# A conditioned convolution / RWKV-7 / product-key layer on one core: order of the second convolution, early second-half activations, loads and stores around the first output projection

## The chip, the core and the metric

The kernel runs on one core of a Trainium2 chip, in one launch. The metric is the device time of an execution in microseconds; what is compared is the median of repeated runs.

The core has five engines with instruction queues of their own: TensorE (PE; its weight loads are listed as PEld), VectorE (DVE), ScalarE (ACT), GpSimd (POOL) and SyncE (SP), which issues nearly all DMAs here. Each engine takes its instructions strictly in the order in which they stand in the program; a DMA waits in SP's queue until what it needs is there, and the DMAs behind it wait too.

## The reference, cut to what matters

```python
mod = silu(c) @ cond_w + cond_b                       # six vectors of 1024: shift1, scale1, gate1, shift2, scale2, gate2
h = layer_norm(x) * (1 + scale1) + shift1             # x: 1024 tokens x 1024
p = h @ w_in                                          # 2816 columns
# group A: 1024 of the columns: gated, a causal depthwise convolution of 31 taps over time, layer norm, silu
u = p[:, :512] * sigmoid(p[:, 512:1024]);  y_conv = silu(layer_norm(conv31(u) + conv_b, g, b))
# group B: 1792 columns: RWKV-7, eight heads of 64
xm = p_rw + (previous token's p_rw - p_rw) * mu;  r, k, v, wd, ad, gd = split(xm)
decay, a, g = f(tanh(wd) @ rw_w2), sigmoid(rw_a0 + ad @ rw_a2), sigmoid(gd) @ rw_g2
kk = k * rw_kk;  kk = kk / max(norm(kk, per head of 64), 1e-12)       # the key norms
k = k * (1 + (a - 1) * rw_ka)
S_t = S_{t-1} diag(w_t) - (S_{t-1} kk_t)(kk_t * a_t)^T + v_t k_t^T;  y_t = S_t r_t
y_rw = (group_norm(y) + sum(r * k * rw_rk) * v) * g
y1 = concatenate(y_conv, y_rw) @ w_out
x1 = layer_norm(2**0.25 * x + gate1 * y1, ln1_g, ln1_b)
# product keys: 8 heads, two halves of 128 keys each, the best 16 of each, the best 16 of their sums
h2 = layer_norm(x1) * (1 + scale2) + shift2;  q = h2 @ peer_wq;  s1, s2 = q @ k1, q @ k2
experts, gates = top 16 of (top 16 of s1 + top 16 of s2), softmax
y2 = sum over the chosen of gelu(h2 . peer_u[e]) * gate * peer_v[e]   # 16384 experts
out = layer_norm(2**0.25 * x1 + gate2 * y2, ln2_g, ln2_b)
```

All is float32. Large products are made of three matmuls over a high and a low part of each operand (`hi`, `lo`, type float32r); smaller ones are plain float32.

## The kernel before, in words

**Stages.** The 1024 tokens are split into two halves of 512 for the input projection and into eight tiles of 128 for the rest.

1. `inproj(0, ...)` works on the first half. `load_x` brings in four tiles of x, `normalize` takes out mean and deviation, `to_channels` transposes a column block of 128 channels for all four tiles on PE, applies shift and scale on ACT (`hf`) and splits the result into the activations `hi` and `lo` (`hhi`, `hlo`; eight blocks each, `k` = 0 to 7). The 22 weight tiles of `w_in` (128 columns each; 24 matmuls of 128x512 for each, `proj`, line 217) are loaded raw, split by ACT and POOL and stored split in DRAM for the second half. `glu` makes the convolution's input and queues `conv(0)`; `products(ct)` and `mixed(ct)`, for four channel groups `ct`, make the operands of the recurrence and store them (`AR_d`, `BK_d`, `v_d`, `bv_d`, `gt_d`). `mixed` makes the key norms: `ones_h`, a block-diagonal matrix of ones, times the squares `sq` on PE gives the sums of squares already spread over the 64 channels of a head; ACT takes the root (`nr`, 128x512), DVE bounds it, takes the reciprocal (line 456) and multiplies.
2. The recurrence runs over 16 steps of 64 tokens: `solve(c)` inverts the step's triangular system (lines 655 to 739), `pass_state(c)` carries the state on (line 760 writes the new state `SN`), `group_norm(j)` finishes 128 tokens at every second step and stores them (`rwkv_d[j]`, line 812).
3. Beside the recurrence runs everything else, as generators in the list `side`: first `inproj(1)` for the second half (its activations are made at its beginning, its `glu` stands at its end), then `front(t0)` for pairs of tiles (loads both groups' outputs, splits them, projects with `w_out`, line 867, adds x, norms twice), then `query(t0)` (`wq`, line 217 with `h2hi`, `h2lo`; the keys' scores, line 939; the best 16 by DVE). `fill()`, called after each few matmuls of the recurrence, steps `side` at a given rate. A second list, `slow`, is stepped once in four fills: the convolutions of both halves, and `choose`, which picks the experts of a tile.
4. `gate_matrix` builds the dense gate matrices of five tiles (masks on DVE, line 1091; matmuls, line 1105) and stores them in DRAM.
5. The expert stage: 32 groups of 512 experts over those five tiles (lines 1388 and 1404), and beside it a gather of single expert rows for the other three tiles.

**What sets the order.** The generators set the program's order, and with it each instruction's priority. A scheduler then places the instructions of every engine: the one of the highest priority that is ready by its own reckoning goes first, and a tile from a pool is given out when a slot is free. The outcome is one fixed list for each engine. What is free or not in the pools therefore decides too: `page(...)` takes from 30 pages of 128x512 (`pgp`), `tp(...)` in `inproj(0)` from 28 others (`tpg`), `mm()` from three PSUM banks, `fe` weights from two buffers.

**Names used below.** `conv(h)` loads its input (`u_d` to `u`), multiplies by taps (`ctap`: made by POOL for the first half and kept in DRAM as `tape_d`; loaded from there for the second), 144 matmuls (line 525), then a norm over channels (lines 534, 543) and its store `conv_d`. `cond_some` brings in rows of `cond_w` (`cw`, 512 KB each, two buffers of the pool `fe`) and DVE multiplies and sums them (line 300) into `mod`. `firsts` lists the generators that have to be finished at step 9, when the pool `fe` is closed. `CD` says whether the second convolution goes to `held` (run from `side`) or to `slow`.

## Time and profile before

| what | value |
|---|---|
| median of 3 runs | 3153.32 us (3149.43 to 3163.98) |
| the profiled execution | 3159.3 us, of which the instructions span 3157.5 us; mean granted clock of TensorE 0.959 |
| PE busy | 2966.5 us, 94% of the span |
| DVE, ACT, POOL busy | 76%, 37%, 57% |
| chain that ended last | PE 52%, DVE 19%, DMA 7% |
| HBM | 800.76 MB read, 141.39 MB written |

The page of the profile gives such totals; the chain is the work that ended last, followed back from the end to what released it. Tables by stage give, for each stretch of the span, its length, the busy time of each engine with its count of records, the granted clock (PEclk, 1.0 is full speed), the busy share of the DMA engines and what they moved. In rows of the timeline the first two numbers are start and length in us, and the bracket at the end is the engine's idle time before the row with what ended it. One float32 matmul of the program leaves two records in the trace, one of type float32r leaves one.

### The profile page before, as it was taken

The page shows a single profiled execution, that of the slowest core. Times are in us where ns is not written, and L with a number is a line of the kernel's source. Part 1 is how long each engine was busy: PE and PEld are TensorE (multiplying, and loading weights), DVE is VectorE, ACT ScalarE, POOL GpSimd, SP SyncE. Part 2 cuts the span into 40 slices and gives each one's busy share as a digit, 9 for nine tenths or more (in the row PEclk, how much of TensorE's full clock was granted, in tenths as well). Part 3 has the DMA queues.
Part 4 walks back from the last instruction along what each step waited for, and adds up shares of the span by engine and source line. Part 5 has one row for each costly group of instructions (what it writes and reads, how often), then busy time and mean ns, then how long its engine had stood idle before and what let it go on. Part 6 is the DMA issues. An engine that isn't in the chain of part 4 may idle for free.

```text
span 3157.5 us, 54845 instructions
## 1 busy us (share of the span) xinstructions
PE 2966.5 (94%) x20416; PEld 2621.4 (83%) x20416; DVE 2388.5 (76%) x5388; ACT 1181.8 (37%) x2220; POOL 1815.5 (57%) x1419
## 2 busy tenths in 40 slices
PE   6979999989899889899999999999999999999996
PEld 4748667878778788898898888889899998999985
DVE  6276654447876989369989999887787877778789
ACT  5552442334345667742332323323222232222323
POOL 2433112224362443477777776877778678777874
PEclk9989999968888999999999999999999999999998
DMA  8878856768576998999999998999999989998995
GB/s 317 308 203 311 261 159 205 267 220 312 201 239 208 310 330 288 292 341 343 312 326 332 318 341 305 341 348 336 345 331 340 341 317 361 327 348 328 339 332 198
DMA packets 441579, 945.77 MB, mean 300 GB/s; under 512 B 92464, under 2 KB 242400, under 8 KB 419296
## 3 DMA queue, kind: packets, MB, share of 16 engines
q1 hardware_dynamic: 248480, 497.62, 45.8%
q0 software_dynamic: 110592, 402.70, 34.9%
q10 hardware_dynamic: 82240, 41.94, 4.8%
q8 instruction: 160, 2.62, 0.3%
q14 instruction: 107, 0.88, 0.1%
HBM read 800.76 MB, written 141.39 MB: 298 GB/s over the span
## 4 chain that ended last, share of the span: by engine, by line
PE 52%; DVE 19%; DMA 7%; issue 6%; POOL 4%; ACT 3%; SPq 0%; another core or an unknown queue 0%; ACTq 0%; POOLq 0%; DVEq 0%
PE mg L1388 18%; PE md L1404 17%; PE mm L217 5%; DVE grow L1267 3%; PE mm L867 2%; POOL grow L1259 2%; PE mm L525 2%; PE mgate L1105 2%; DVE gy L1274 2%; DMA cw<-cond_w 1%; DVE yacc L1422 1%; DMA grow<-peer_u,eid 1%; DVE mask L1091 1%; DMA vraw<-peer_vt 1%; DMA grow<-peer_v,eid 1%
## 5 line engine op out<-in xcount | busy, mean ns | idle before, releaser
L1388 PE MATMUL mg<-h2h,uhi 128*128 128x320 f32 x2024 | 626.9, 310 | 7.1 <-DVE al L1394 7.1
L1388 PE MATMUL mg<-h2h,ulo 128*128 128x320 f32 x2024 | 625.8, 309 | 1.8 <-POOL ulo L1304 1.6
L1388 PE MATMUL mg<-h2l,uhi 128*128 128x320 f32 x2024 | 626.0, 309 | 0.0
L1274 DVE SCALAR_TENSOR_TENSOR gy<-grow,gz,gy 128x1024 f32<-128x1024 f32 x381 | 487.7, 1280 | 18.0 <-DMA grow<-peer_v,eid 16.4
L1404 PE MATMUL md<-vhi,ah 128*128 128x512 f32 x1260 | 486.5, 392 | 5.8 <-ACT ah L1393 2.8
L1404 PE MATMUL md<-vlo,ah 128*128 128x512 f32 x1260 | 491.8, 391 | 0.0
L1404 PE MATMUL md<-vhi,al 128*128 128x512 f32 x1260 | 491.3, 391 | 0.0
L1267 DVE SCALAR_TENSOR_TENSOR grow<-grow,gh 128x1024 f32<-128x1024 f32 x384 | 460.8, 1211 | 36.9 <-DMA grow<-peer_u,eid 32.9
L1259 POOL DMA_INDIRECT grow<-peer_u,eid x384 | 362.5, 944 | 196.3 <-DVE grow L1267 73.7
L1259 POOL DMA_INDIRECT grow<-peer_v,eid x384 | 367.4, 957 | 185.3 <-DVE gy L1274 89.3
L1388 PEld LDWEIGHTS mg<-h2h,uhi 128*128 128x128 f32 x2024 | 380.4, 188 | 15.1 <-DVE al L1394 10.0
L1388 PEld LDWEIGHTS mg<-h2l,uhi 128*128 128x128 f32 x2024 | 380.4, 188 | 5.4
L1388 PEld LDWEIGHTS mg<-h2h,ulo 128*128 128x128 f32 x2024 | 380.3, 188 | 5.5 <-POOL ulo L1304 2.7
L1304 POOL TENSOR_TENSOR ulo<-uraw,uhi 128x1024 fp32r<-128x1024 f32 x128 | 310.0, 2422 | 34.8 <-ACT uhi L1302 29.1
L1304 POOL TENSOR_TENSOR vlo<-vraw,vhi 128x1024 fp32r<-128x1024 f32 x128 | 308.9, 2414 | 10.6 <-ACT vhi L1302 5.4
L1302 ACT ACTIVATE vhi<-vraw 128x1024 fp32r<-128x1024 f32 x128 | 135.2, 1056 | 425.1 <-DMA vraw<-peer_vt 382.7
L1422 DVE TENSOR_TENSOR yacc<-md,yacc 128x512 f32<-128x512 f32 x300 | 204.2, 685 | 115.9 <-PE md L1404 104.3
L1404 PEld LDWEIGHTS md<-vhi,ah 128*128 128x128 f32 x1260 | 236.5, 188 | 53.8 <-ACT ah L1393 4.3
L1404 PEld LDWEIGHTS md<-vlo,ah 128*128 128x128 f32 x1260 | 236.9, 188 | 49.1
L1098 POOL TENSOR_TENSOR ob<-mask,selt 128x384 f32<-128x384 bf16 x160 | 140.9, 894 | 237.9 <-DVE mask L1091 105.3
L1404 PEld LDWEIGHTS md<-vhi,al 128*128 128x128 f32 x1260 | 237.0, 188 | 45.2
L217 PE MATMUL mm<-hhi,wsplit 128*128 128x512 f32 x672 | 228.7, 414 | 8.4 <-ACT gsig L396 5.4
(415 smaller groups left out, 5660.6 us busy)
## 6 DMA issues: line engine op xcount, KB each, us to landing
uraw<-peer_ut SPq DMA_DIRECT2D x128, 512.0 KB
vraw<-peer_vt SPq DMA_DIRECT2D x128, 512.0 KB
wsplit<-split_wq SPq DMA_DIRECT2D x48, 1024.0 KB
G_d<-stage ACTq DMA_DIRECT2D x20, 2048.0 KB
gmat<-G_d SPq DMA_DIRECT2D x32, 1024.0 KB
cw<-cond_w SPq DMA_DIRECT2D x48, 512.0 KB
wsplit<-split_w_out SPq DMA_DIRECT2D x24, 1024.0 KB
split_w_in<-wsplit SPq DMA_DIRECT2D x22, 1024.0 KB
```

Of the source, the lines that this page charges most:

```text
L217: T.matmul(pt, l[:, k, :], r[k], start=i == 0, stop=i == 3 * KD - 1)
L525: T.matmul(pt[:, 128 * g:128 * g + 128], dg[:, 128 * j:128 * j + 128], ubuf[ct][:, g, LAGS - 1 - m:LAGS - 1 - m + 128], start=m == 0, stop ...
L867: T.matmul(acc[t], l[k][:, ts], r, start=k == 0 and q == 0, stop=k == KD - 1 and q == 2)
L1098: G.tensor_mul(ob[:, :3], mb[:, :3], gt[:, c:c + 3, None].to_broadcast([128, 3, 128]))
L1259: G.indirect_dma_start(out=r, out_offset=None, in_=peer_u if k < 128 else peer_v, in_offset=bass.IndirectOffsetOnAxis(ap=eid[:, k % 128:k ...
L1267: V.scalar_tensor_tensor(r, r, 1.0, ht, op0=OP.mult, op1=OP.mult, accum_out=z[:, i:i + 1])
L1274: V.scalar_tensor_tensor(y, r, z[:, i - 128:i - 127], y, op0=OP.mult, op1=OP.add)
L1302: A.activation(hi, raw, AF.Copy)
L1304: G.tensor_sub(lo, raw, hi.bitcast(F32))
L1388: T.matmul(p, l[:, k, :], r[k][:, bs], start=i == 0, stop=i == 3 * KD - 1)
L1404: T.matmul(p, l[:, ts], r[:, e % 2, :], start=e == 0 and q == 0, stop=e == 3 and q == 2)
L1422: ins = V.tensor_add(ya, p, ya)
```

## The change

Five edits. (1) `CD = 1`: the second convolution no longer stands in `slow` but in `side`, behind `front(0)` and ahead of `query(0)`; at step 9 it is among what has to be finished. (2) In `front`, for pairs whose tiles all go to the dense stage (the first two pairs), the rows `ln1_g` and `ln1_b` are loaded ahead of the projection instead of behind it. (3) `group_norm` writes to a tile `yk[j]` in SBUF and `front` reads that; `rwkv_d` is gone, with 8 stores of 256 KB and 16 loads of 128 KB. (4) `second_half`, stepped from within `inproj(0)` at the counts in `EARLY`, loads, norms and transposes the second half's x; `inproj(1)` finds its activations in `acts`. `hf` and x take their slots from `tpg` there. (5) In `mixed`, the sums of squares are made with `sq` as the weights (four matmuls of 128x2), the root and the reciprocal are taken on 128x8, ACT spreads them over the 64 channels (`wide`), and four matmuls with the identity turn them back.

```diff
-CD = 0
+CD = 1
+EARLY = (24, 144, 156) + tuple(range(168, 168 + 8 * 12, 12))
...
-    rwkv_d = dt([4, 128, 128], "rwkv_d", 8)
...
-            hf = page("hf", w=n)
+            hf = pg_("hf")[:, :n]
...
+    acts = []
+    def second_half(ps, pg_):
+        tp = lambda name: pg_.tile([128, 512], F32, tag="pg", name=name)
+        bank = lambda: ps.tile([128, 512], F32, name="m2")
+        xn = [load_x(4 + i, tp) for i in range(4)]
+        yield
+        for i, parts in enumerate(xn):
+            normalize(parts, parts)
+            if i % 2:
+                yield
+        acts[:] = [], []
+        for k in range(KD):
+            for a_, n_ in zip(acts, ("hhi", "hlo")):
+                a_.append(page(n_, F32R))
+            to_channels(xn, lambda k: mod[:, k:k + 1], lambda k: modp[:, k, 0:1], *acts, None, (k,), bank, tp)
+            yield
...
-        if h == 0:
+        if h == 1:
+            hi, lo = acts
+        else:
+            hi = [page("hhi", F32R) for _ in range(KD)]
+            lo = [page("hlo", F32R) for _ in range(KD)]
...
-        else:
-            for g in range(2):
-                xn = []
-                for i in range(2):
-                    parts = load_x(4 * h + 2 * g + i, tp)
-                    normalize(parts, parts)
-                    xn.append(parts)
-                sl = slice(256 * g, 256 * g + 256)
-                to_channels(xn, shift, scale, [t[:, sl] for t in hi], [t[:, sl] for t in lo])
-                yield
...
             pn = m2()
-            T.matmul(pn, ones_h, sq, start=True, stop=True)
-            nr = tp("nr")
-            A.activation(nr, pn, AF.Sqrt)
+            for t in range(4):
+                T.matmul(pn[:, 2 * t:2 * t + 2], sq[:, 128 * t:128 * t + 128], ones_h[:, 0::64], start=True, stop=True)
+            inv = sq[:, 0:8]
+            A.activation(inv, pn[:, 0:8], AF.Sqrt)
+            V.tensor_scalar_max(inv, inv, 1e-12)
+            V.reciprocal(inv, inv)
+            wide = tp("wide")
+            A.activation(wide.rearrange("p (a b) -> p a b", b=64), inv[:, :, None].to_broadcast([128, 8, 64]), AF.Copy)
+            for t in range(4):
+                T.matmul(pn[:, 128 * t:128 * t + 128], wide[:, 128 * t:128 * t + 128], ident, start=True, stop=True)
...
-            V.tensor_scalar_max(nr, nr, 1e-12)
-            V.reciprocal(nr, nr)
-            kkn = nr
-            V.scalar_tensor_tensor(kkn, k_, col("kk", ct), nr, op0=OP.mult, op1=OP.mult)
+            kkn = wide
+            V.scalar_tensor_tensor(kkn, k_, col("kk", ct), pn, op0=OP.mult, op1=OP.mult)
...
-        drain(inproj(0, tps, tpg))
+        ahead = second_half(tps, tpg)
+        for n_, _ in enumerate(inproj(0, tps, tpg)):
+            if n_ in EARLY:
+                next(ahead)
+        drain(ahead)
...
-        G.tensor_mul(yo, yo, gg)
-        ld(rwkv_d[j].rearrange("g p t -> p g t"), yo)
+        if j < 6:
+            yk[j] = rw.tile([128, 4, 128], F32, name="yk", bufs=2)
+        else:
+            yk[j] = page("yk").rearrange("p (g t) -> p g t", g=4)
+        G.tensor_mul(yk[j], yo, gg)
...
-        for i in range(KD // 2):
+        for i in (2, 3, 0, 1):
...
-                for t in range(nt):
-                    ld(f[:, :, 128 * t:128 * t + 128],
-                       rwkv_d[tile0 + t][2 * i - 4:2 * i - 2].rearrange("g p t -> p g t"))
...
+            for t in range(nt):
+                ts = slice(128 * t, 128 * t + 128)
+                f = yk[tile0 + t][:, 2 * i - 4:2 * i - 2]
+                A.activation(h_[:, :, ts], f, AF.Copy)
+                G.tensor_sub(l_[:, :, ts], f, h_[:, :, ts].bitcast(F32))
...
+        if not any(fetch):
+            row_loads(("g1", ln_rows[0]), ("b1", ln_rows[1]))
         for i in range(2):
             acc = [mm() for _ in range(nt)]
...
+        if any(fetch):
+            row_loads(("g1", ln_rows[0]), ("b1", ln_rows[1]), ("sh2", mod_d[3]), ("sc2", mod_d[4]))
...
         if c == 9:
+            while any(f in side for f in firsts[:2 + CD]):
+                step(side)
             while conv_left and slow:
                 slow_step(1)
-            while any(f in side for f in firsts[:2 + CD]):
-                step(side)
```

The three places below are those of which the prediction speaks. Rows name the line, the operation, out<-in by the program's names, the size and how many follow each other.

The first is TensorE at the end of the first half's projection. The 528th and last of its matmuls is the single row of line 217 with `hhi` just ahead of the other lines; line 255 transposes the second half's x, 473 makes the bonus, 424 to 432 the small products of `products`, 442 the sums of squares. Before:

```order
L217 MATMUL mm<-hlo,wsplit 128x512
L217 MATMUL mm<-hhi,wsplit 128x512
L255 MATMUL mm<-ident,xt 128x128 x16
L473 MATMUL m_1264<-sq,ones_h 128x512
L424 MATMUL m_1388<-lw,w2a_t 128x512
L428 MATMUL m_1392<-lw,w2a_t 128x512
L432 MATMUL m_1396<-sg,g_t 128x512
L442 MATMUL m_1403<-sq,ones_h 128x512
L255 MATMUL mm<-ident,xt 128x128 x12
```

In the changed program, where lines have shifted (460 is the second of the two new sets of matmuls of the key norms), from the last matmul of the first half on:

```order
L217 MATMUL mm<-hhi,wsplit 128x512
L460 MATMUL m_1410<-ident,wide 128x128 x4
L217 MATMUL mm<-hhi,wsplit 128x512
L217 MATMUL mm<-hlo,wsplit 128x512
L217 MATMUL mm<-hhi,wsplit 128x512 x2
```

The second half's 32 transposes have moved up among the matmuls of the first half (all stand ahead of the first small products), and the second half's projection follows the first's at once, after four small matmuls.

The second place is DVE in the first half's first `mixed`. Before (460 and 461 make the mixed key, 446 the running sum, 447 and 453 belong to the decays, 455, 456 and 458 to the key norms, 259 to the second half's activations, 383 to the projection's tiles):

```order
L460 TENSOR_SCALAR sq<-a,colt 128x512
L446 SCALAR_TENSOR_TENSOR cum<-mask_182,sig 128x512
L461 SCALAR_TENSOR_TENSOR sq<-sq,xm 128x512
L455 TENSOR_SCALAR nr<-nr 128x512
L447 TENSOR_TENSOR sig<-cum,sig 128x512
L453 COPY wc_73<-W 128x8
L456 RECIPROCAL nr<-nr 128x512
L383 SCALAR_TENSOR_TENSOR xm<-pshift,colt,xm 128x512 x2
L259 TENSOR_TENSOR hlo<-hf,hhi 128x256
L458 SCALAR_TENSOR_TENSOR nr<-xm,colt,nr 128x512
```

Now (455 and 456 are the bound and the reciprocal on eight columns, 472 multiplies by the spread norms from PSUM):

```order
L455 TENSOR_SCALAR sq<-sq 128x8
L456 RECIPROCAL sq<-sq 128x8
L462 SCALAR_TENSOR_TENSOR cum<-mask_174,sig 128x512
L474 TENSOR_SCALAR sq<-a,colt 128x512
L463 TENSOR_TENSOR sig<-cum,sig 128x512
L475 SCALAR_TENSOR_TENSOR sq<-sq,xm 128x512
L469 COPY wc_73<-W 128x8
L392 SCALAR_TENSOR_TENSOR xm<-pshift,colt,xm 128x512 x2
L472 SCALAR_TENSOR_TENSOR wide<-xm,colt,m_1237 128x512
```

The wide reciprocal has left DVE's list, and the second half's `hlo` rows no longer stand between.

The third place is SP's queue around `front(0)`. Before (the gate's row, x, the first nine taps of the second convolution, then the weights `w_out`):

```order
L855 DMA row_gate<-mod_d 128x512 x2
L322 DMA xt<-x 128x512 x4
L517 DMA ctap<-tape_d_89 128x512 x9
L207 DMA split_w_out_4649<-wsplit 128x2048
L189 DMA wraw<-w_out 128x1024
```

Now, at the same place, and further down where the taps have gone (924 stores the pair's x1):

```order
L880 DMA row_gate<-mod_d 128x512 x2
L322 DMA xt<-x 128x512 x4
L889 DMA row_g_4651<-ln_rows 128x512
L889 DMA row_g_4652<-ln_rows 128x512
L889 DMA row_b_4655<-ln_rows 128x512
L889 DMA row_b_4656<-ln_rows 128x512
```

```order
L924 DMA x_d_97<-xt 128x512 x2
L681 DMA bkl<-BK_d_80 128x4x192
L924 DMA x_d_98<-xt 128x512 x2
L531 DMA ctap<-tape_d_89 128x512 x9
L683 DMA vl<-v_d_82 128x4x64
```

The four row loads have moved from behind the projection to ahead of the weights, and the taps from ahead of the projection to behind the pair's last store.

More of the change, by code (lines that the diff above doesn't have):

```diff
@@ L247, in normalize, with to_channels @@
             A.activation(d_, s_, AF.Identity, bias=b, scale=r)
-    def to_channels(xn, shift, scale, hi, lo, keep=None, ks=range(KD), bank=None):
+    def to_channels(xn, shift, scale, hi, lo, keep=None, ks=range(KD), bank=None, pg_=page):
         n = 128 * len(xn)
@@ L332, in tp @@
             return pg_.tile([128, 512], F32, tag="pg", name=name)
-        tok = slice(HALF * h, HALF * h + HALF)
         xn = []
-        hi = [page("hhi", F32R) for _ in range(KD)]
-        lo = [page("hlo", F32R) for _ in range(KD)]
         shift, scale = lambda k: mod[:, k:k + 1], lambda k: modp[:, k, 0:1]
         first = []
-        if h == 0:
+        if h == 1:
[3 more added lines that the diff above has]
+            lo = [page("hlo", F32R) for _ in range(KD)]
             for i in range(4):
@@ L349, in inproj @@
                 V.tensor_scalar_add(modp[:, k, 0:1], mod[:, 8 + k:9 + k], 1.0)
-                to_channels(xn, shift, scale, hi, lo, None, (k,), m2)
+                to_channels(xn, shift, scale, hi, lo, None, (k,), m2, tp)
                 for (whi, wlo), pt in two:
@@ L834, in front @@
         lp, lo = duo("yclo", F32R, pg_)
[L835 to L836 removed]
+        for i in (2, 3, 0, 1):
+            h_, l_ = hp[i], lp[i]
             if i < 2:
+                f = pg_("ycf").rearrange("p (a t) -> p a t", a=2)
                 c = t0 % HALF // PH
@@ L856, in front, with row_loads @@
         xts = [load_x(tile0 + t, pg_) for t in range(nt)]
+        rows = {}
+        def row_loads(*srcs):
+            for nm, src in srcs:
+                rows[nm] = [pg_("row_" + nm) for _ in range(2)]
+                s_ = src.rearrange("a b -> (a b)") if len(src.shape) == 2 else src
+                for i in range(2):
+                    ld(rows[nm][i], s_[512 * i:512 * i + 512][None, :].to_broadcast([128, 512]))
+        if not any(fetch):
+            row_loads(("g1", ln_rows[0]), ("b1", ln_rows[1]))
         for i in range(2):
```

17 lines of the change are left out of this document (5 added, 12 removed).

## The prediction

> **What bounds the kernel now.** I read the table by stage first, cut at places that the work itself sets: 175 and 214 are the ends of two streaks of projection matmuls, 535, 618, 776 and 987 the ends of the recurrence's steps 5, 6, 10 and 15, 1300 the start of the expert stage.
>
> ```profile
> core 0: us, PE busy (x) PEld busy (x) DVE busy (x) ACT busy (x) POOL busy (x), PEclk, DMA share, GB/s
> 60.00:175.00 115.00, 114.19 (x477) 88.37 (x475) 31.10 (x45) 57.97 (x100) 45.87 (x20) 0.99 0.92 312
> 175.00:214.00 39.00, 17.99 (x49) 7.49 (x47) 31.96 (x57) 28.79 (x58) 6.77 (x6) 0.61 0.57 166
> ...
> 535.00:618.00 83.00, 82.62 (x837) 72.98 (x836) 36.37 (x64) 23.77 (x49) 22.23 (x11) 0.97 0.78 283
> 618.00:776.00 158.00, 141.88 (x1655) 121.08 (x1654) 86.54 (x289) 66.36 (x135) 57.15 (x37) 0.79 0.78 264
> 776.00:987.00 211.00, 190.95 (x2073) 168.69 (x2072) 162.12 (x680) 85.89 (x193) 89.25 (x84) 0.87 0.66 219
> 987.00:1300.00 313.00, 275.96 (x2150) 262.07 (x2149) 258.25 (x1028) 211.69 (x479) 125.33 (x132) 0.96 0.91 300
> 1300.00:3157.00 1857.00, 1811.67 (x10182) 1646.30 (x10180) 1534.74 (x2715) 553.38 (x930) 1378.40 (x1052) 0.99 0.91 327
> ```
>
> The expert stage, 1857 of 3157 us, has PE busy 98% at full clock, and no edit touches it: what the change is worth is how much sooner that stage begins. The stages ahead of it are PE's too, but leaky. Busy time by clock is the work at full speed; what a stage has beyond that is lost: 39 - 18.0 x 0.61 = 28 us in the hole from 175 to 214, 46 us from 618 to 776 (158 - 141.9 x 0.79), 45 from 776 to 987, 48 from 987 to 1300. The stage from 535 to 618 loses 3. Since PE has the same matmuls to run after the change but for a few, **an edit gains only what it takes out of these losses**; work that moves from one stage to a later one moves time with it.
>
> The steps' ends are the rows of the instruction that writes the state (all 16, then steps 6 and 10):
>
> ```profile
> L760 DVE TENSOR_TENSOR SN<-SN,bank x16: 375/412/422, 330.1 to 986.2; 128x256 f32<-128x256 f32 x16
> L760 DVE TENSOR_TENSOR SN<-SN,bank x1: 408/408/408, 617.3 to 617.3; 128x256 f32<-128x256 f32 x1
> L760 DVE TENSOR_TENSOR SN<-SN,bank x1: 410/410/410, 775.8 to 775.8; 128x256 f32<-128x256 f32 x1
> ```
>
> **The early activations.** PE's timeline shows what is in the hole; the second view is DVE's.
>
> ```profile
> 174.88 0.40 PE L217 MATMUL mm<-hhi,wsplit 128*128 128x512 f32 x1
> 176.62 1.02 PE L255 MATMUL mm<-ident,xt 128*128 128x128 f32 x4 [1.35 <-ACT xm L382]
> 197.00 2.08 PE L442 MATMUL m<-sq,ones_h 128*128 128x512 f32 x2 [3.89 <-ACT sq L440]
> 208.82 0.90 PE L255 MATMUL mm<-ident,xt 128*128 128x128 f32 x3 [9.11 <-ACT xt L247]
> 213.93 0.48 PE L217 MATMUL mm<-hhi,wsplit 128*128 128x512 f32 x1
> ...
> 193.95 1.33 DVE L225 BATCH_NORM_STATS2 bnst<-xt 128x6 f32<-128x512 f32 x2 [3.10 <-DMA xt<-x]
> 202.44 3.34 DVE L456 RECIPROCAL nr<-nr 128x512 f32<-128x512 f32 x1
> 206.67 1.25 DVE L245 SCALAR_TENSOR_TENSOR nbias<-bnmv,rstd 128x1 f32<-128x1 f32 x1
> ```
>
> The last tiles of x land at 193.95, their norm waits on DVE behind a reciprocal, and PE stands 9.11 us for it. The new order puts the transposes into the first half, and the next projection matmul stands right behind the last. The transposes remain PE's work. So the hole's 28 us go. What is late next: the 16 pages of the first half and 16 of the second are 32, and there are 30, so the last block's pair is copied only after the first half's last matmul; that copy stands on ACT and the subtraction on DVE behind the small work of `mixed`, and three matmuls of the next tile, with all of PE behind them, wait for both: 0 to 2.5 us, I take 1. SP now carries four more x loads (1 MB) past the weights of the first half. In the stage from 60 to 175 the DMAs are 0.92 busy; were they the limit, 1 MB at 312 GB/s would be 3.3 us, but PE is busy 114.19 of 115, so 0 to 3.3 and I take 1. **Term: -28 + 2.**
>
> **The key norms.**
>
> ```profile
> L456 DVE RECIPROCAL nr<-nr 128x512 f32<-128x512 f32 x8 | 26.7, 3342 | 0.0
> ...
> 368.62 3.26 DVE nr L456
> 413.86 3.26 DVE nr L456
> ...
> 214.05 1.28 ACT L444 ACT_TABLE_LOAD   x1
> 215.34 0.60 ACT L444 ACTIVATE nr<-m 128x512 f32<-128x512 f32 x1
> ...
> 908.17 1.09 PE mgate L1105 x8
> 965.63 0.58 PE bank L730 x16
> ```
>
> DVE is relieved of eight reciprocals, 26.7 us; two of them lie on the chain (368.62 and 413.86). On PE, 1.0 us for the old 128x512 product goes (2.08 at half clock, row 197.00). The four spreading matmuls of 128x128 come for the eight records of 1.09 us that the gate's four take. The four of two columns have no row: at most those 1.09, at least half of the 0.58 that sixteen narrow records of the recurrence take (965.63); I take 0.6. So PE pays 0.7 for each of eight, +5 for all. ACT gets a copy of 0.6 and saves some 0.4 on the root, beside other work (ACT is busy 58 of 115 us in the stage from 60). The chain's two reciprocals are replaced by that copy, the spreading matmuls and two tiny DVE operations, 2 us or so: -2 x 1.3 = -3. A wait is added: PE stands for `wide`, and behind it all its matmuls. In the first half's last groups 14 projection matmuls (114.19 / 477 = 0.24 us a record in the stage from 60, 3.4 us) cover a table load of 1.28, a root, two DVE operations and the copy, 2.7 us and the hops, so 0 to 2 us a time; eight times 0.4 is +3. **Term: +5.**
>
> **Rows ahead, y kept.** The chain of waits around the first pair's norm:
>
> ```profile
> 627.21 5.57 DMA row_b<-ln_rows
> 633.15 4.48 DMA row_b<-ln_rows
> 660.25 2.47 DMA rwkv_d<-yo
> 662.74 3.36 DMA ycf<-rwkv_d
> ...
> 667.21 0.37 PE L756 MATMUL bank<-UVe,BKe 128*64 128x64 f32 x1 [4.32 <-ACT UVo L752]
> ```
>
> The row loads cost the chain 10.05 us; PE had the recurrence to run meanwhile, so of these 0 to 10 I take half, -5. The way of y through DRAM costs 5.83, and PE's wait of 4.32 us at 662.9 falls into it (ACT's copy stood behind that of `ycf`): 0 to -6, I take -4. Moving the row loads ahead puts 1 MB in front of the first weights of `w_out` on SP's queue, some 4 us there; it is in the -5. The 24 DMAs that vanish free a queue that isn't the limit there. For the later pairs the rows stay where they were. **Term: -9.**
>
> **The second convolution.** Counting TensorE's list up to each step tells where work has gone. At step 6 the old order has all of `conv(1)` behind it and 82 matmuls of line 867, the new one none of `conv(1)` and 64; at step 10 the old one 192 of line 867 and 216 of the query, the new one 96 and none (it has run the convolution since); at step 15 669 of the query, 288 of line 867 and 80 gates, against 504, 228 and 4. The prices:
>
> ```profile
> 535.00:618.00 83.00, 35.64 (x288) 34.29 (x288) 0.97 0.78 283
> 987.00:1300.00 313.00, 122.64 (x864) 110.86 (x864) 0.96 0.91 300
> 987.00:1300.00 313.00, 26.38 (x96) 18.27 (x96) 0.96 0.91 300
> 987.00:1300.00 313.00, 127.97 (x925) 118.30 (x926) 0.96 0.91 300
> ```
>
> (the stage's time of line 525 alone, then 217, 867 and 1105). So 35.6 us of the convolution with some 8 of its norm and 18 x 0.275 leave the dense stage from 535 to 618, 49 us; by step 10 the new order is 96 x 0.275 + 216 x 0.142 + 4 = 61 behind, and at step 15 165 x 0.142 + 60 x 0.275 + 76 x 0.277 = 61. Step 15 comes that much sooner and the stage behind it is that much longer: 0 net. Between steps 6 and 10 the fill beside the recurrence is some 54 us instead of 69, so the stage should take 143 instead of 158. Its loss could be filled by the convolution, which needs neither norms nor DRAM's y, -25 (half of its 46), or grow: a step took 16 us at full clock and 35 at half:
>
> ```profile
> 618.00:634.00 16.00, 14.31 (x241) 11.38 (x239) 10.18 (x35) 12.22 (x24) 8.17 (x7) 1.00 0.80 227
> 634.00:669.00 35.00, 26.19 (x340) 22.43 (x342) 18.29 (x58) 14.60 (x36) 12.32 (x12) 0.52 0.63 193
> 646.00:662.00 16.00, 16.00 (x217) 13.79 (x217) 7.79 (x20) 7.87 (x19) 5.33 (x6) 0.50 0.50 141
> ```
>
> Four steps of 35 and 54 of fill are 194, +51. Against that, the taps are loaded only once the first pair's x1 has been stored (they wait for pages), and the query waits behind the convolution; for it, the first pair's own work is done sooner. Between -25 and +51 I take 0, since both orders have a thin stretch, only at other steps. In the last stage PE, DVE and DMA are all near 0.9; packing 61 us more there may cost a tenth more, 0 to 6, I take 5. **Term: +5.**
>
> Here the Trainium skill is weighed. The row 646 to 662 has PE busy all 16.00 us, and its clock at 0.50 throughout: the recurrence's small matmuls do not bring the clock back. The Trainium skill's page "TensorE: Matmul & The Clock Gate", section "Part 1: The HAM clock gate (the "warmup" mystery)", says that the default clock is half and that about 3.4 us of sustained matmuls lift it to full. By that rule a stretch of recurrence alone would run at full clock, four steps of 16 and 54 of fill would be 118 us, and the sum would come out 25 us lower than mine. The trace disagrees in that row, so I keep the thin stretch dear; the rule's outcome is the second rival below.
>
> **The sum**: -28 + 2 + 5 - 9 + 0 + 5 = -25 us, against the profiled execution's own 3159.3. That execution stands 6 us above the median of 3153.3, which I take as the base: 3153 - 25 = **3128 us**.
>
> **The rivals.**
> - *The hole is covered* (no change): DVE's sums of the conditioning rows set the pace behind it.
>
> ```profile
> 299.37 5.03 DMA cw<-cond_w
> 361.17 4.26 DMA cw<-cond_w
> ```
>
> These two (the first and the last of eight such DMA pieces on the chain from 299 to 366) stand for 32 rows of `cond_w` through two buffers. If that pipeline, not PE, sets step 1, the hole's 28 us turn into DVE's wait for DMA: 3128 + 28 = 3156. Against it: the rows are released by the last `mixed` of the first half, which comes sooner as well, and the hole's DMA share of 0.57 leaves room.
> - *The losses are filled* (more): the convolution takes half of the 46 us of the stage from 618 to 776: 3103. For it: its 144 matmuls are dense. It is also what the clock rule would give.
> - *The thinned stretch starves* (slower): steps 6 to 10 run at half clock as 634 to 669 did: +51, 3179. It decides from a stage of 143 + 25 + 16 = 184 us on. For it: the taps and the query both come late. Against it: step 11 needs none of that work, so it should only shift it.
>
> **How the numbers follow.** My forecast, 3128 with 3112 to 3140 as its own range, gets 0.45; covered 0.23; filled 0.20; starved 0.12. The runs before lie within 3149 to 3164, so about 0.5% (16 us) is what a measurement can tell from no change. Faster than 3137 are most of the forecast (0.38), all of filled and a little of covered: 0.60. Slower than 3169 is most of starved: 0.10. The range runs from a little below filled, 3092, to a little above covered, 3164, and leaves out starved and the ends.
>
> **What would show it.** Right: no gap of PE over 4 us between the two halves' projections, step 0 near 300 us instead of 331 and step 15 near 900, no reciprocal of 3.3 us, a stage from step 6 to 10 of about 143 us, the start of the expert stage near 1275, the expert stage unchanged at 1857. Wrong: step 0 at its old time with DVE waiting for `cw`; a clock near 0.5 from step 6 to 10; or a last stage that grows by more than the 61 us moved into it.

## The result, and the profile after

| | us (median of its runs) | against before |
|---|---|---|
| before | 3154.18 (3149.43 to 3163.98) | |
| after | 3178.29 (3174.02 to 3183.19) | 1.0077, 95% interval 1.0056 to 1.0098 |
| predicted | 3128 (3092 to 3164) | |

The change makes the kernel 24 us slower, and the time lies outside the range. The profiled execution of after took 3178.91 us (span 3177.1), that of before 3159.3 (3157.5).

The table by stage of after, cut at the same places of the work: 183 is the end of the first half's projection, 341, 520, 564, 694 and 937 the ends of the steps 0, 5, 6, 10 and 15, 1312 the start of the expert stage. Below it the rows of the instruction that writes the state (all 16 steps), and of the gates' matmuls, before and after:

```profile
183.00:341.00 158.00, 145.95 (x1150) 118.53 (x1149) 104.24 (x201) 62.84 (x128) 59.55 (x48) 0.96 0.89 286
341.00:520.00 179.00, 172.40 (x1854) 132.38 (x1855) 93.91 (x212) 64.58 (x127) 19.75 (x18) 0.88 0.56 161
520.00:564.00 44.00, 37.73 (x423) 28.23 (x421) 27.20 (x47) 19.37 (x36) 19.78 (x13) 0.88 0.89 300
564.00:694.00 130.00, 118.45 (x1678) 105.55 (x1678) 62.60 (x170) 42.76 (x100) 26.76 (x21) 0.88 0.53 178
694.00:937.00 243.00, 204.73 (x2092) 176.08 (x2089) 161.22 (x691) 82.35 (x172) 101.46 (x81) 0.83 0.66 228
937.00:1312.00 375.00, 328.08 (x2484) 308.93 (x2483) 288.54 (x1148) 241.55 (x544) 145.78 (x154) 0.93 0.87 287
1312.00:3177.00 1865.00, 1817.28 (x10224) 1651.51 (x10223) 1535.24 (x2721) 561.51 (x947) 1383.36 (x1058) 0.99 0.91 328
```

```profile
L779 DVE TENSOR_TENSOR SN<-SN,bank x16: 382/413/421, 340.8 to 936.8; 128x256 f32<-128x256 f32 x16
```

```profile
L1105 PE MATMUL mgate<-oa,ob x1280: 270/275/583, 900.4 to 1337.6; 128*128 128x128 f32 x183
```

```profile
L1136 PE MATMUL mgate<-oa,ob x1280: 270/275/554, 930.4 to 1363.5; 128*128 128x128 f32 x183
```

Read the lengths of the stages one after the other. Up to step 10 the new order is ahead: step 5 at 520 instead of 535, step 10 at 694 instead of 776, and the stage from step 6 to 10 takes 130 us instead of 158. Of the 82 us by which step 10 comes sooner, though, some 54 are work that now stands behind it (TensorE has done 578 us of work by then instead of 632, by the count explained below); only the rest is loss saved. Then the stage from step 10 to 15 takes 243 instead of 211: its loss (length less busy time by clock) is 243 - 204.7 x 0.83 = 73 us where it was 45, and the gates begin 30 us later. The last stage takes 375 instead of 313: by the same count its work grew by 47 us (311 against 264) and its loss by 15. The expert stage starts at 1312 instead of 1300, and its table row is 8 us longer; these 8, of some 20 between the two profiled executions, were not traced further.

For the comparison of kernels I use the loss of TensorE, the time that its busy time by clock doesn't cover, added up microsecond by microsecond between the same events (so summed it comes out a few us lower than from a stage's mean clock). The rest of the span, busy time by clock, is nearly the same: 2873 us in before, 2878 in after. In each line the losses are those of one profiled execution, which can lie 10 us or more off the kernel's median (e7: span 3147.5, median 3157.3; the widest is e15, told below, with 3216.8 against 3202.8); differences of a few us between losses mean nothing. Under "end" stands all that follows the start of the expert stage.

| kernel (label) | median | ratio to before, 95% | to step 0 | 0 to 5 | 5 to 10 | 10 to 15 | to experts | end |
|---|---|---|---|---|---|---|---|---|
| before | 3154 | | 70 | 29 | 46 | 42 | 49 | 45 |
| after | 3178.3 | 1.0077 (1.0056-1.0098) | 55 | 28 | 33 | 68 | 64 | 47 |
| after, no conv move (e1) | 3163.8 | 1.0029 (1.0014-1.0044) | 55 | 27 | 46 | 34 | 80 | 41 |
| before + conv move (e2) | 3180.6 | 1.0093 (1.0070-1.0116) | 72 | 19 | 45 | 57 | 54 | 58 |
| ... and query ahead (e12) | 3165.2 | 1.0035 (1.0020-1.0049) | 72 | 27 | 35 | 61 | 40 | 55 |
| before + acts (e7) | 3157.3 | 1.0013 (0.9999-1.0027) | 72 | 27 | 51 | 41 | 45 | 42 |
| before + acts, norms (e11) | 3149.5 | 0.9986 (0.9971-1.0002) | 53 | 22 | 47 | 45 | 51 | 47 |
| after, late acts (e4) | 3193.3 | 1.0128 (1.0101-1.0154) | 68 | 17 | 38 | 63 | 62 | 58 |
| after, old norms (e3) | 3171.6 | 1.0063 (1.0044-1.0081) | 76 | 24 | 35 | 58 | 54 | 55 |
| before + y, rows (e8) | 3178.5 | 1.0080 (1.0055-1.0104) | 69 | 27 | 40 | 40 | 79 | 46 |
| before + y of six, rows (e9) | 3171.4 | 1.0058 (1.0040-1.0077) | 72 | 21 | 40 | 43 | 67 | 44 |
| before + rows (e13) | 3185.7 | 1.0115 (1.0100-1.0129) | 73 | 20 | 51 | 56 | 56 | 48 |
| before + y of six (e14) | 3143.8 | 0.9981 (0.9964-0.9997) | 71 | 23 | 38 | 39 | 43 | 43 |
| after, y by DRAM (e5) | 3171.3 | 1.0061 (1.0038-1.0083) | 56 | 23 | 37 | 63 | 56 | 52 |
| after, rows behind (e6) | 3164.8 | 1.0040 (1.0025-1.0056) | 60 | 17 | 32 | 64 | 70 | 44 |
| after, y of six (e10) | 3167.0 | 1.0043 (1.0027-1.0058) | 58 | 16 | 33 | 61 | 60 | 46 |
| acts, norms, y of six (e16) | 3148.0 | 0.9979 (0.9962-0.9997) | 57 | 20 | 55 | 37 | 58 | 42 |
| ... + conv move (e17) | 3164.1 | 1.0034 (1.0018-1.0049) | 54 | 28 | 32 | 62 | 69 | 43 |
| e16, gates held back (e18) | 3172.1 | 1.0068 (1.0044-1.0092) | 57 | 19 | 54 | 50 | 72 | 40 |

### The profile page after: what moved, and what is told of

It is laid out like the page before. It is cut to its first block, busy times and chain, and to the rows that moved or that the text cites. A ratio compares the mean times of both kernels' runs of the same rounds, so it can differ in the third digit from the quotient of the medians.

```text
span 3177.1 us, 55060 instructions
## 1 busy us (share of the span) xinstructions
PE 2976.1 (94%) x20528; PEld 2638.4 (83%) x20528; DVE 2361.3 (74%) x5380; ACT 1179.9 (37%) x2219; POOL 1816.7 (57%) x1427
## 4 chain that ended last, share of the span: by engine, by line
PE 41%; DVE 11%; DMA 4%; issue 3%; POOL 1%; ACT 1%; SPq 0%; DVEq 0%; POOLq 0%; ACTq 0%
PE mg L1419 20%; PE md L1435 19%; DVE gy L1305 2%; DVE grow L1298 2%; DVE yacc L1453 1%; PE mm L217 1%; PE mgate L1136 1%; DMA grow<-peer_v,eid 1%; DMA G_d<-stage 1%; DMA grow<-peer_u,eid 1%; POOL grow L1290 1%; DMA vraw<-peer_vt 1%; DVE mg L1423 1%; DVE al L1425 0%; POOL ulo L1335 0%
## 5 line engine op out<-in xcount | busy, mean ns | idle before, releaser
L205 POOL TENSOR_TENSOR wsplit<-wraw,wsplit 128x1024 fp32r<-128x1024 f32 x46 | 112.3, 2444 | 209.5 <-ACT wsplit L204 193.7
```

What stands on the lines that cost most here:

```text
L205: G.tensor_sub(lo, raw, hi.bitcast(F32))
```

## The experiments

Each edit changes the whole list of each engine, since the scheduler places everything anew; so edits were taken out of after and put into before, and the traces were read at the same events. The medians of before were between 3149 and 3154 on the chips used; each ratio is against the runs of before on the same chip. The intervals are some 5 us to either side, so prices below that are not told from nothing.

**The second convolution.** Taken out of after (e1), put into before alone (e2):

```diff
-CD = 1
+CD = 0
...
+            while conv_left and slow:
+                slow_step(1)
             while any(f in side for f in firsts[:2 + CD]):
                 step(side)
-            while conv_left and slow:
-                slow_step(1)
```

> The changed kernel with the second convolution back in the list that is stepped once in four fills (and the old order of the two loops at step 9); the other four edits stay. Theory A (the convolution's move is what costs: it puts off the first query, so that its choosing of keys on DVE falls on steps 13 to 15, where TensorE then has nothing to fill with; stage from step 10 to 15 243 us against 211 before): the loss of 32 us goes, 3178 - 32 = 3146 us or below, and the stage from step 10 to 15 comes back to 211 within 12. Theory B (the move only shifts work, as the prediction had it, and the loss comes from the early activations and the key norms): 3178 within 10.

> The kernel before with the second convolution's move alone (CD = 1 and the swapped loops at step 9). Theory A: it costs by itself what it costs in the changed kernel, 3154 + 32 = 3186 us, with the first query some 30 us later than step 10 and a longer stage from step 10 to 15. Theory B: 3154 within 10.

Measured: 3163.8 and 3180.6. The move costs 28 us alone and 14 within after. Theory A has the place right: from step 10 to 15 after loses 68 us and e1 34, e2 57 and before 42. It has not the size in after (3146 or below was expected), since e1 loses 13 us more from step 5 to 10 and 16 more on the way to the expert stage. Theory B, that the move only shifts work, is out: its 3178 and 3154 were both missed. The first step of theory A was tested by the query queued ahead of the convolution (e12), and then by the third pair's front put behind the second pair's query (e15, the kernel of e2 with `AHEADF = ()`):

```diff
-            if c == 3 and CD:
-                side.append(run(held))
-                firsts.append(side[-1])
             if c < 11:
                 side.append(query(64 * (c - 3)))
                 firsts.append(side[-1])
+            if c == 3 and CD:
+                side.append(run(held))
+                firsts.append(side[-1])
```

> The kernel before with the second convolution in the side list (as in the second run, 3181), but queued behind the first pair's query instead of ahead of it. Theory A (it is the late query that costs, since its choosing falls on steps 13 to 15 and the gates come too late to fill them): the loss of TensorE from step 10 to 15 goes back from 57 us to 42 or so, and the time to 3153 to 3163. Rival (the convolution in the side list costs in itself, wherever it stands): 3181 within 8.

> The kernel before with the second convolution in the side list (as in the second run, 3181), and the third pair's front queued behind the second pair's query instead of ahead of it. Theory A in its second form (from step 10 to 15 TensorE lacks work because the choosing is late for the gates and the third pair's front stands ahead of the second pair's query): the query fills the steps and the loss from step 10 to 15 goes from 57 to 45 or less; but the third pair comes later (its rows stand behind 17 loads of wq in SP's queue instead of 5), so that the loss from step 15 to the expert stage grows by 10 or more, and the time is 3175 to 3195. Rival (these steps lose because the recurrence's chain itself is longer there, DVE being shared with the choosing): the loss from step 10 to 15 stays at 57 within 6.

Measured: 3165.2 for e12, so the query's place is worth 15 of the 28 us; but the loss from step 10 to 15 stayed at 61, where theory A asked for 42, and the gain came before and behind it. The time lies just outside what theory A gave and far from its rival's 3181. The first query ran from 622 us, and yet the choosing of its second tile ended only at 888 (905 in e2, 867 in before). e15 took 3202.8 us (1.0162, 1.0147 to 1.0178): the loss from step 10 to 15 came down a little, to 50, where 45 or less was expected, and that before the expert stage rose to 102, from 54; the third pair came late. The time is above the range expected, and the profiled execution is a long one, so 102 is rather high. What is put into these steps is missing behind them.

The move's price by a single difference, without the other faults, and the gates alone (e16 and e17 differ in `CD` and the two loops; in e18 the only edit to e16 is `GSTEP = 1 << 20`, by which no gate is stepped beside the recurrence):

> The same with the second convolution in the side list (the changed kernel without its rows ahead and without the two pages). If its price holds without the other faults: 15 (as it came out of the changed kernel) to 28 (as alone) above the other kernel of this call, 3155 to 3168, with a loss of TensorE of 55 us or more from step 10 to 15. If the price needed them: within 6 of the other kernel.

> The kernel of the sixteenth run (second convolution where it was) with the gate matrices held back until the recurrence's last step is done; before, 192 of their matmuls stood ahead of step 15. Theory A in its last form (what the convolution's move costs is that the choosing, and with it the gates, come too late to fill the steps 10 to 15): the loss of TensorE there goes from 37 us to 55 or more, as in the seventeenth run (62), and the time from 3148 to 3158 or more. Rival (the gates are not what is missing there; other work takes their place): loss within 8 of 37 and 3148 within 6.

The stages of e16 and then of e17, each from step 5 to 10, 10 to 15, and to the expert stage, with the gates' rows of e16, e17 and e18:

```profile
513.00:794.00 281.00, 251.22 (x2770) 219.97 (x2771) 147.96 (x503) 109.77 (x225) 92.66 (x57) 0.88 0.77 271
794.00:966.00 172.00, 155.18 (x1766) 133.31 (x1765) 137.42 (x505) 75.14 (x172) 83.46 (x85) 0.86 0.60 192
966.00:1307.00 341.00, 294.50 (x2294) 279.55 (x2293) 264.77 (x1069) 228.86 (x518) 136.03 (x145) 0.95 0.90 298
```

```profile
517.00:690.00 173.00, 158.09 (x2098) 135.30 (x2099) 91.09 (x218) 62.06 (x136) 47.88 (x33) 0.87 0.63 211
690.00:910.00 220.00, 184.39 (x2028) 160.62 (x2026) 152.56 (x682) 76.87 (x161) 87.63 (x63) 0.82 0.67 232
910.00:1310.00 400.00, 349.33 (x2598) 326.19 (x2598) 300.27 (x1163) 255.98 (x573) 166.04 (x178) 0.93 0.89 296
```

```profile
L1137 PE MATMUL mgate<-oa,ob x1280: 270/275/582, 876.7 to 1326.1; 128*128 128x128 f32 x183
```

```profile
L1136 PE MATMUL mgate<-oa,ob x1280: 270/275/582, 926.5 to 1346.6; 128*128 128x128 f32 x183
```

```profile
L1137 PE MATMUL mgate<-oa,ob x1280: 270/275/582, 982.8 to 1351.8; 128*128 128x128 f32 x183
```

Measured: e17 3164.1 against e16's 3148.0, 16 us. Follow the loss through the three stages: from step 5 to 10 it falls from 281 - 251.2 x 0.88 = 60 to 173 - 158.1 x 0.87 = 35, so the convolution does fill the losses there, by 25 us. From step 10 to 15 it rises from 172 - 155.2 x 0.86 = 39 to 220 - 184.4 x 0.82 = 69, and on the way to the expert stage from 61 to 75: +30 and +14. What was gained is given back nearly twice over. The gates begin at 927 in e17 and at 877 in e16, because the choosing of the first two tiles ends 46 and 41 us later. With the gates alone held back (983, e18), with the convolution in its old place, the kernel took 3172 us, 24 more than e16, and lost 50 us from step 10 to 15 by the finer count, where e16 lost 37 and e17 62. In e16 192 records of the gates (96 matmuls) stand ahead of step 15, in e17 and e18 none. So holding the gates out costs more than the whole move, and 13 us of it in these steps; of the 25 us that e17 loses more there, missing gates account for about 13. The rest of it is open, and theory A in its last form, which asked for a loss of 55 or more in e18, is half right.

**Rows ahead, y kept.** Each taken out of after (e5: y goes through `rwkv_d` again; e6: `row_loads` for all pairs behind the projection), and both put into before (e8):

> The changed kernel with y stored in DRAM by the group norm and loaded again by the output projection, as before. Theory C (what is left over: taking the other edits' prices from the first four runs, 28 for the convolution alone, 7 for the key norms, -15 for the activations, the 26 us of loss leave +6 for y and the rows, and by the convolution's price out of the changed kernel, 14, even +20; the kept y takes two pages from the later pairs): 3178 - 6 to - 20, that is 3158 to 3172. The prediction's term (y through DRAM costs 4 us): 3182. Neither: 3178 within 4.

> The changed kernel with the rows of the first two pairs' norms loaded behind the projection, as before. Theory C with the rows as the cause (their 1 MB stands ahead of the first weights of w_out): 3158 to 3172. The prediction's term (rows ahead save 5 us): 3183. Neither: 3178 within 4.

> The kernel before with y kept in SBUF and the rows ahead, without the other three edits. Theory C: 3153 + 6 to + 20. The prediction's term: 3153 - 9 = 3144. Neither: 3153 within 4.

Measured: 3171.3, 3164.8 and 3178.5. This was the largest surprise: a term forecast at -9 costs 26 us alone, more than the 6 to 20 that theory C gave it. Where, the last columns say: 79 us of loss between step 15 and the expert stage instead of 49. The third pair's rows on SP and its first norm product on DVE, in before and then in e8 (its residual's second halves are the `xt<-xt,mm` rows):

```profile
890.73 0.86 SPq L878 DMA_DIRECT2D row_g<-ln_rows  x2
```

```profile
925.46 1.37 DVE L871 SCALAR_TENSOR_TENSOR xt<-xt,mm 128x512 f32<-128x512 f32 x2
...
934.18 3.05 DVE L885 TENSOR_TENSOR xt<-xt,row_g 128x512 f32<-128x512 f32 x3
```

```profile
957.80 1.91 SPq L870 DMA_DIRECT2D row_g<-ln_rows  x2
```

```profile
940.02 1.38 DVE L888 SCALAR_TENSOR_TENSOR xt<-xt,mm 128x512 f32<-128x512 f32 x2
985.97 5.36 DVE L897 TENSOR_TENSOR xt<-xt,row_g 128x512 f32<-128x512 f32 x4
```

The rows are issued 67 us later, and the norm's first product comes 46 us after the residual instead of 9. Not all of it is a wait for the rows: they land 8.8 us after their issue, by 968, and from there the product stands behind the group norm in DVE's list. In SP's list the rows stood behind 10 loads of `wq` instead of 5. Theory D has it that the kept y of tiles 6 and 7 takes two of the 30 pages just when these rows need eight. So y was kept for the first six tiles only, with the rows ahead in before (e9), and in after (e10):

```diff
         if j < 6:
             yk[j] = rw.tile([128, 4, 128], F32, name="yk", bufs=2)
+            G.tensor_mul(yk[j], yo, gg)
         else:
-            yk[j] = page("yk").rearrange("p (g t) -> p g t", g=4)
-        G.tensor_mul(yk[j], yo, gg)
+            G.tensor_mul(yo, yo, gg)
+            ld(rwkv_d[j].rearrange("g p t -> p g t"), yo)
```

> The kernel before with the rows ahead and y kept in SBUF for the first six tiles only; tiles 6 and 7, whose kept y takes two of the 30 pages, go through DRAM as before. Theory D (the loss of y and rows alone, 26 us, is a matter of pages: with the two pages gone the third pair's norm rows get their slots late and stand on SP behind 10 loads of wq and 16 of w_out instead of 5 and 13, so that its norm came at 987 us, 81 us after its residual, where before it took 35): the rows stand at their old place again, the wait from residual to norm is 35 within 8, and the time 3153 within 8. Rival (the first pair's rows ahead of w_out, or the kept y's copies on ACT and POOL): 3170 to 3180.

> The changed kernel with y kept for the first six tiles only. Theory D: the third pair's rows come back to their old place in SP's queue, which took 7 us (y through DRAM) and 13 us (rows behind) out of the changed kernel: 3165 to 3171. Rival (the pages are not it): 3178 within 4.

Measured: the rows are back at their old place, the wait from the residual's first rows to the norm is 41 us (81 in e8, 35 in before), and e10 gains 11 us on after. But e9 still took 3171.4, in the range of theory D's rival (3170 to 3180). So theory D has the place of the third pair's rows right, and the two pages are worth 11 us in after, but at most 7 of the 26 us in before, where the two intervals overlap. Then each alone:

> The kernel before with the rows of the first two pairs' norms loaded ahead, nothing else. What is left of y and rows once the pages of tiles 6 and 7 are out of it is 18 us (3171 against 3153). Theory F (the rows ahead carry it: four pages stand from ahead of the projection to the norm, and 1 MB on SP's queue ahead of the first w_out): 3165 to 3171. Rival (they cost nothing here, y's six tiles do): 3153 within 5. By the prediction's term: 3148.

> The kernel before with y kept for the first six tiles, the rest through DRAM, rows where they were. Theory F: 3153 within 5, or 3149 if the way through DRAM was worth the prediction's 4 us. Rival (the kept tiles carry the 18 us): 3165 to 3171.

Measured: 3185.7 and 3143.8. The rows ahead alone cost 36 us, twice what theory F expected and more than together with the kept y, and the kept y gains 5.5 us (ratio 0.9981, so 1 to 11 us). The first pair's second residual, its norm's first product and, for before, the last sums with `row_b`, before and then with the rows ahead (e13):

```profile
625.76 1.39 DVE L871 SCALAR_TENSOR_TENSOR xt<-xt,mm 128x512 f32<-128x512 f32 x2
632.64 1.40 DVE L885 TENSOR_TENSOR xt<-xt,row_g 128x512 f32<-128x512 f32 x2 [0.45 <-ACT xt L247]
637.76 3.70 POOL L886 TENSOR_TENSOR xt<-xt,row_b 128x512 f32<-128x512 f32 x3 [2.59 <-DMA row_b<-ln_rows]
```

```profile
624.36 1.37 DVE L882 SCALAR_TENSOR_TENSOR xt<-xt,mm 128x512 f32<-128x512 f32 x2 [1.50 <-PE mm L878]
631.29 0.69 DVE L891 TENSOR_TENSOR xt<-xt,row_g 128x512 f32<-128x512 f32 x1 [0.56 <-ACT xt L247]
```

It is 7 us from the residual to the norm's first product in both: `row_g` never held it up, ACT's normalizing did. The last row of `row_b` did hold POOL up, by 2.59 us; but from the start of the residual to the end of the last sum it is 15.7 us before and 14.7 in e13, so hardly anything was there to gain. What was lost shows later, from 880 to 980 us (before, then e13):

```profile
880.00:980.00 100.00, 96.65 (x1053) 83.94 (x1053) 67.93 (x209) 47.68 (x106) 45.03 (x51) 0.91 0.70 227
```

```profile
880.00:980.00 100.00, 94.31 (x902) 78.06 (x903) 58.85 (x162) 40.00 (x90) 45.86 (x51) 0.79 0.57 190
```

PE is about as busy, at 0.79 of the clock instead of 0.91: 14 us less work. The gates and the third pair's residual both come 14 us later there (914 instead of 900). Why a list with the row loads ahead puts them later isn't shown; four pages are held through the projection, but no run gave them back alone.

The price of the rows ahead hangs on what stands beside them: 36 us in before, some 24 on top of the kept y of six tiles (e9 against e14), 13 within after (e6), and 3, which is not told from nothing, within after once the two pages are given back (e10 against e17). The first pair's rows on SP, before, in e13, and in e6, whose program has them behind the projection:

```profile
627.21 0.43 SPq L878 DMA_DIRECT2D row_b<-ln_rows  x1
523.97 0.95 SPq L864 DMA_DIRECT2D row_b<-ln_rows  x2
520.36 1.47 SPq L903 DMA_DIRECT2D row_b<-ln_rows  x2
```

In e6 they are issued early all the same, as in e2 and e17 (at 524 and 523). With the second convolution in `side`, its taps no longer stand there in SP's list, and the scheduler itself moves the first pair's rows to the place that the edit gives them. So in after it is the convolution's move as much as edit (2) that has put the four row loads ahead of the weights; within after, edit (2) moves only the second pair's ahead, from 760 to 720 us.

**Activations and key norms.** Taken out of after (e3, e4), put into before (e7: activations, e11: both):

> The changed kernel with the key norms made as before (one 128x512 product, root and reciprocal on 128x512). Theory A says nothing of them: by the prediction's sum they cost 5 us, so 3173, within 8 of 3178. Theory B (the added waits on TensorE and ACT in the projection are what eats the early activations' gain, since step 5 came only 15 us sooner where 26 were forecast): 3160 or below, with step 5 at 510 or below instead of 520.

> The changed kernel with the second half's activations made at the start of the second half's projection, as before. If the early activations gain what they took at step 5 (15 us): 3178 + 15 = 3193. If they gain the whole hole as forecast, 28: 3206. If they are covered by the rows of cond_w and gain nothing at the end: 3178 within 8. If they harm: below 3170.

> The kernel before with the early activations alone. If the 15 us that they are worth in the changed kernel hold alone: 3153 - 15 = 3138. As predicted, the hole's 28 less 2: 3127. If the recurrence, which starts no sooner (its first matmuls stand at 259 us before and 256 after), only runs with less beside it, and what fills the hole is missing later: 3153 within 8.

> The kernel before with the early activations and the compact key norms, without the other edits. Theory E (the two belong together: with the old reciprocals of 3.3 us on DVE, step 0 of the recurrence went from 331 us to 356 and the activations alone gained nothing; with the compact norms it stands at 341 and the activations are worth 15 us in the changed kernel): loss up to step 0 some 55 us against 70, work of TensorE some 4 more, time 3153 - 10 = 3143 within 5. Rival (the recurrence sets the pace whatever is done ahead of it): 3153 within 5. Rival (the norms cost 7 wherever they are): 3157 + 7 = 3164.

Measured: 3171.6, 3193.3, 3157.3 and 3149.5. The activations are worth 15 us in after and nothing alone. The norms cost 7 us in after and gain 8 on top of the activations; both pairs of intervals overlap, the second barely. For e11, theory E had the loss up to step 0 right (53, some 55 expected) and not the time: 3143 within 5 was its forecast, and 3149.5 lies in the range of its first rival. The product that ends each `mixed` (first half: the row with `m`), before, in e7 and in after, and under each the first matmul of the recurrence:

```profile
L474 DVE TENSOR_TENSOR sq<-m,xm x4: 677/684/691, 164.8 to 233.5; 128x512 f32<-128x512 f32 x4
```

```profile
L672 PE MATMUL bank<-arl,bkl x256: 271/272/580, 258.6 to 891.7; 64*128 64x128 f32 x128
```

```profile
L485 DVE TENSOR_TENSOR sq<-m,xm x4: 691/692/692, 172.9 to 250.9; 128x512 f32<-128x512 f32 x4
```

```profile
L687 PE MATMUL bank<-arl,bkl x256: 271/272/579, 267.6 to 884.0; 64*128 64x128 f32 x128
```

```profile
L488 DVE TENSOR_TENSOR sq<-m,xm x4: 676/691/692, 171.1 to 236.8; 128x512 f32<-128x512 f32 x4
```

```profile
L691 PE MATMUL bank<-arl,bkl x256: 272/272/580, 255.7 to 810.4; 64*128 64x128 f32 x128
```

The hole of PE was the time in which `mixed` ran, and the recurrence, whose operands `mixed` stores in DRAM, follows the last `mixed` by 25, 17 and 19 us. Work put into the hole makes `mixed` later: by 17 us with the old reciprocals, by 3 with the compact norms. So without the convolution's move the two belong together; step 0 stands at 356 us in e7, at 340 in e11. That is still later than the 331 of before, though the recurrence begins 3 or 4 us sooner: step 0 itself takes 85 us instead of 72, and why was not traced. By its end TensorE has done 26 us more work in after than in before (286 against 260).

**Those that did not lose, together:**

> The edits that did not lose: early activations, compact key norms, y kept for the first six tiles; rows where they were, the second convolution where it was. If they add up (3149 - 4 for the first two by the eleventh run, - 5.5 for y by the fourteenth, each against its own runs of before): 3140 within 5, faster than both kernels. If the scheduler's list eats one of them: 3144 to 3153.

Measured: 3148.0, ratio 0.9979 (0.9962 to 0.9997), faster than both kernels, if by 0.2%. The gains didn't add up: e14's y alone gives as much.

Six of these kernels form a path from before to after with one edit between neighbours. By the ratios, in us:

| edit added | kernel | price of the step | sum |
|---|---|---|---|
| early activations | e7 | +4 | +4 |
| compact key norms | e11 | -8 | -4 |
| y of six tiles kept | e16 | -2 | -7 |
| second convolution moved | e17 | +17 | +11 |
| rows ahead | e10 | +3 | +14 |
| y of tiles 6 and 7 kept in pages | after | +11 | +24 |

Another order of the edits gives other prices, as the rows show. And no run made a new list without a real edit, so how much the time changes merely because the scheduler places everything anew is not known; prices of a few us may be no more than that.

## Why the prediction was wrong, point by point

The sum missed by 50 us, and along the path above three of its terms share that. The activations with the norms, -26 and +5, came to -4: 17 too hopeful. The convolution with the packing, 0 and +5, came to +17: 12 too hopeful. Rows and y, -9, came to +12: 21 too hopeful.

- **What bounds the kernel.** Right: PE ahead of the expert stage, which hardly changed (1865 against 1857), and the time went with the losses. What was left out is that a loss filled at one place can open at the next.
- **The early activations, -28 + 2.** The hole is gone; PE goes from one half's projection into the other's:

```profile
182.57 0.40 PE L217 MATMUL mm<-hhi,wsplit 128*128 128x512 f32 x1
182.81 1.06 PE L460 MATMUL m<-ident,wide 128*128 128x128 f32 x8
183.85 0.50 PE L217 MATMUL mm<-hhi,wsplit 128*128 128x512 f32 x1
```

  But step 0 came at 341 us, not near 300, and step 5 15 us sooner, not 26: mis-sized by half in after, and with nothing left of it alone (e7). The rival "the hole is covered" had the right consequence for e7, by another cover: DVE's `mixed`. Whether the rows of `cond_w` cover some of it too isn't shown; no run changed them, and the last of them was issued at 356 us in after, 364 in before.
- **The key norms, +5.** The size fits in after (7), but the sign is the other one without the convolution's move (-8), so that is luck in part. The matmuls with two columns were put at 0.6 us for four; the timeline has 1.05 us for them, as much as the 1.06 of the spreading ones (row 182.81 above), so PE pays (1.05 + 1.06 - 1.0) x 8 = 9 us. No reciprocal of 3.3 us on 128x512 is left, as forecast.

```profile
327.85 1.05 PE L452 MATMUL mgate<-ones_h,sq 128*128 128x2 f32 x8
```

- **Rows ahead, y kept, -9.** The step that failed worst. The way of y through DRAM came out near its size (4 forecast; 5.5 alone and 2 on the path, for six tiles), within wide intervals. The row loads stood in the chain of waits with 10 us, but the norm's first product wasn't waiting for them and POOL's sum only 2.6 us, with 1 us to gain; and what two more pages taken, and four held longer, do to later loads wasn't priced at all. It is 11 us for the two pages in after and 3 to 36 for the rows.
- **The second convolution, 0 between -25 and +51.** It isn't 0: 14 to 28. Both ends' mechanisms were there, one after the other: the losses from step 6 to 10 were filled (stage of 130, forecast 143; by the prediction's own counts of work behind, 49 us at step 6 and 61 at step 10, the forecast should have been 146), and a thin stretch starved, but from step 10 to 15, which the sum carried over at 211 us and which took 243. The work behind at step 15 was counted; that the choosing and the gates follow it, and that steps 10 to 15 then lack the gates, wasn't.
- **Packing, +5.** The last stage took 375 us, where 313 + 61 + 5 is 379. The sum is near by luck: the work there grew by 47 us, not 61, and the loss by 15, not 5.
- **The rivals.** "Starves" gave 3179, which is the time measured, but by luck: its mechanism stood at the wrong steps, and its deciding stage of 184 us took 130.
- **The clock.** By the clock rule the stage from step 6 to 10 would have been 118 us with the same fill. It was 130. The recurrence's small matmuls still ran at half clock with PE fully busy in two stretches of after (in the second with transposes among them, and with `w_out`'s matmuls from 709.9 us on):

```profile
594.00:606.00 12.00, 12.00 (x132) 0.50 0.66 215
701.00:713.00 12.00, 12.00 (x67) 0.50 0.41 117
```

  The Trainium skill's page "TensorE: Matmul & The Clock Gate", section "Part 1: The HAM clock gate (the "warmup" mystery)", has about 3.4 us of sustained activity lift the clock; these rows, as the one in the prediction, disagree for these small matmuls.

## What to carry to other kernels

A hole of one engine is worth filling only if the chain that ends it gets no longer. Look first at who works in it, and relieve that engine in the same edit. In a kernel whose list is made by a scheduler, a filler that is moved up is missing where it stood, and so is all that waits behind it: follow it to the next consumers (here the choosing and the gates), and price the thin stretch that it leaves. Count the buffers that an early load or a kept tile holds, and who needs them then; a load that hardly anything waits for isn't worth a page. And an edit's price, measured once, holds for the list that it was measured in: the same row loads cost between 3 and 36 us.

## What was not expected of the hardware

Eight records of float32 matmuls with 2 columns took 1.05 us of PE, eight with 128 columns 1.06 (rows 327.85 and 182.81 above; the former took 0.95 to 1.05 in all eight places): with new weights for each, making a product narrow saved next to nothing. And a kernel with four row loads moved up by some hundred us, and four more by 50, took 1.15% more time, and the views read here show no wait that names them.
